# Values of the band and of the memory as products of 512 weight columns, in weight pieces of two feature tiles

## The chip, the cores and the metric

One core of one Trainium2 chip runs the kernel. The metric is the device time of one execution in microseconds. Three executions of the kernel before gave 1246.0, 1249.38 and 1249.93 us; the median, 1249.38 us, is the time before.

## The reference, cut to what matters

The program is one layer of an encoder trunk for 512 tokens of 1024 features, all in float32. Two token mixers work on the same normalised input h: a gated delta rule with 8 heads (A) and a band attention with 16 heads (B). Their outputs are merged, then follow a cross-attention into 256 memory tokens with 4 heads, a feed-forward part and a last norm. The two products that the change touches are the value projection of the band, and the value half of the memory projection:

```
h = rmsnorm(x, norm_mix[l])
qa, ka, va, za, alpha, beta, qb, kb, vb, ga, gb = _split_cols(h @ w_in[l], IN_SPLITS)   # vb: 512 x 1024
...
ob = _chunk_band_attention(qb, kb, vb, band_bias)
...
kk, vv = _split_cols(memn @ w_kv, (M_HEADS * M_DH, M_HEADS * M_DH))                     # vv: 256 x 1024
```

## The kernel before, in words

**Products.** Each float32 operand is kept as two parts, hi and lo, in a reduced format of the same width, and each product of a feature tile is three matmuls: hi by hi, lo by hi, hi by lo. `split` (L113) makes the parts: ScalarE copies into hi (L114), VectorE or GpSimd subtracts for lo (L116, or L118 with a scale). `weights` (L121) loads a piece of weights with a DMA on SP's queue (raw) and splits it (whi, wlo); each of the three has 3 buffers of 1024 columns, so a piece is at most 512 KB.

Most products are made by `block_steps` (L131): 128 weight columns stand in TensorE, and all 512 tokens move through. The result is transposed, features by tokens. Values are wanted the other way, tokens by features, and are made by `natural` (L149): it loads two pieces of four feature tiles each for 256 output columns, and then for each tile of 128 tokens opens one PSUM bank and makes 8 x 3 matmuls, in which the activations stand and the 256 weight columns move (L165 to L167). After every second feature tile (six matmuls) it yields; after the eighth it hands the bank to `evac`.

**Who uses natural here.** `vb_all` (L654) makes the values of the band: four groups of 256 columns, four token tiles each, so 64 yields. Its evac copies 256 columns with ScalarE into a buffer (vbt, three buffers, tag "c") and writes them to DRAM scratch dvb with a DMA on SP's queue (L659); after `proj_a` they are loaded back. `mem_v` (L890) makes the values of the memory: four groups, two token tiles; its evac splits 256 columns into hi and lo of the tile mv. `z_group` uses natural too and is not part of the change.

**PSUM.** Three tags share the eight banks: "mm" with 3 (PM), "ms" with 2 (PS), "sd" with 3 (PD). A new tile waits until the bank it is given has been read out.

**The order of the work.** TensorE's order is the order of the program text; the other engines' orders and the buffers are laid out by a planner with a simulated timeline. `drive` (L176) runs a generator of products and, at each of its yields, first `advance`s every pending generator by one step, then adds rate to a counter due, which starts at -delay x rate, and makes one step of the side generator for each whole unit in it.

The band values run with the output steps of the eight delta-rule heads as the side (L703): rate 1.5, delay 6. A head (`head_out`, L458) takes seven steps: (1) oU, four matmuls into a PS bank; (2) oS, three matmuls into the other PS bank; (3) ScalarE and VectorE read both out; (4) ScalarE squares and sums; (5) VectorE and GpSimd make the factor f (L483, L484), then two waits (5, 6); (7) VectorE scales four tiles into zs (L489), a DMA brings a gate (L492), and `oa_tile` of the head before (L501) transposes its zs into a PS bank (oaT, L506), which ScalarE (oah) and VectorE (oal, L118) read out. The first head has no oaT and takes six; the last takes six waits more and then its own oaT. Pending beside them are the last parts of q6 and q7 (`q_after`, L431): the convolution that reads the bank of q (three steps on VectorE, L351), nine waits, a step qn with four transposes into a PS bank, a step in which ScalarE squares it (L444) and VectorE makes fe (L446), and a step kq with four matmuls into a PS bank that VectorE reads into PT (L454). Ahead of the band values stand the products q5, q6 and q7, which use the three PM banks in turn; behind them `proj_a` (L809), which uses PM banks and takes its weights w_a, eight pieces, over SP's queue.

The memory values stand between the memory keys (`mk`, products of 256 memory tokens) and the queries of the first cross-attention head (L1039), with no side.

Of the kernel before, what the change touches and what calls it, by code (L numbers as in the profile page):

```python
# [9 lines left out]
F32R = mybir.dt.float32r  # L10
AF = mybir.ActivationFunctionType
# [3 lines left out]
P = 128  # L15
T = 512
D = 1024
KD = 8
NT = 4
# [20 lines left out]
def hybrid_block(  # L40
# [5 lines left out]
    nc = tc.nc  # L46
# [19 lines left out]
    def G(tag, name, dt=F32):  # L66
        return up.tile([P, T], dt, tag=tag, bufs=SLOTS[tag], name=nm(name))
# [6 lines left out]
    def TMP(name, tag, bufs=None, shape=(P, T), dt=F32, pool=None):  # L74
        return (pool or tp).tile(list(shape), dt, tag="t" + tag, bufs=bufs or TB[tag], name=nm(name))
# [37 lines left out]
    def split(hi, lo, src, scale=None, eng=None):  # L113
        nc.scalar.activation(hi, src, AF.Copy, scale=1.0 if scale is None else scale)  # L114
        if scale is None:
            (eng or nc.vector).tensor_tensor(out=lo, in0=src, in1=hi.bitcast(F32), op=ALU.subtract)  # L116
        else:
            nc.vector.scalar_tensor_tensor(out=lo, in0=src, scalar=scale, in1=hi.bitcast(F32),  # L118
                                           op0=ALU.mult, op1=ALU.subtract)
# [29 lines left out]
    def natural(src, width, act, ntok, evac, eng=None):  # L149

        w = [weights(src[hf], 4, width, eng) for hf in range(2)]
        for tt in range(ntok):
            ps = PM("nat")
            for k in range(KD):
                natural_step(ps, w[k // 4], k % 4, width, act, tt, k)
                if k % 2:
                    yield
            evac(tt, ps)

    def natural_step(ps, w, kw, width, act, tt, k):  # L160
        tok = slice(tt * P, (tt + 1) * P)
        hi, lo = w
        xh, xl = act[k]
        o = ps[:, :width]
        nc.tensor.matmul(out=o, lhsT=xh[:, tok], rhs=hi[:, kw, :], start=(k == 0), stop=False)  # L165
        nc.tensor.matmul(out=o, lhsT=xl[:, tok], rhs=hi[:, kw, :], start=False, stop=False)  # L166
        nc.tensor.matmul(out=o, lhsT=xh[:, tok], rhs=lo[:, kw, :], start=False, stop=(k == KD - 1))  # L167

    pending = []

# [5 lines left out]
    def drive(*items, side=None, delay=0, rate=1.0):  # L176

        due = -delay * rate
        for steps, after in items:
            for _ in steps:  # L180
                advance()
                due += rate
                while side is not None and due >= 1:
                    due -= 1
                    next(side, None)
            if after is not None:
                pending.append(after)
        if side is not None:
            for _ in side:
                advance()  # L190
# [267 lines left out]
    def head_out(hd):  # L458

        on, ss = kT[hd], SM("ss", 4)  # L460
        pu_, pq = PS("oU"), PS("oS")
        for n in range(NT):
            c = slice(n * P, (n + 1) * P)
            nc.tensor.matmul(out=pu_[:, c], lhsT=PT[hd][:, c], rhs=vs[hd][:, c], start=True, stop=True)
        yield
        for n in range(1, NT):
            c = slice(n * P, (n + 1) * P)
            nc.tensor.matmul(out=pq[:, c], lhsT=qT[hd][:, c], rhs=S[hd, n - 1], start=True, stop=True)
        yield
        for n in range(NT):  # L470
            c = slice(n * P, (n + 1) * P)
            if n > 0:
                nc.scalar.activation(on[:, c], pq[:, c], AF.Copy, scale=eG[:, n, hd : hd + 1])
            else:
                nc.scalar.activation(on[:, c], pu_[:, c], AF.Copy)
        nc.vector.tensor_tensor(out=on[:, P:], in0=pu_[:, P:], in1=on[:, P:], op=ALU.add)
        yield
        for n in range(NT):
            junk = TMP("junk", "junk", 2, (P, P), pool=ap)
            nc.scalar.activation(junk, on[:, n * P : n * P + P], AF.Square, accum_out=ss[:, n : n + 1])  # L480
        yield
        f = SM("f", 4)
        nc.vector.scalar_tensor_tensor(out=f, in0=ss, scalar=4.0 / P, in1=fe[hd], op0=ALU.mult, op1=ALU.add)  # L483
        nc.gpsimd.tensor_tensor(out=f, in0=f, in1=mhalf, op=ALU.pow)  # L484
        yield from wait(2)
        z = zs[hd // 2]
        zc = slice((hd % 2) * P, (hd % 2) * P + P)
        for n in range(NT):
            nc.vector.scalar_tensor_tensor(out=z[:, n, zc], in0=on[:, n * P : (n + 1) * P], scalar=f[:, n : n + 1],  # L489
                                           in1=z[:, n, zc], op0=ALU.mult, op1=ALU.mult)  # L490
        s = sga[hd] = G("b", "sga")
        nc.sync.dma_start(out=s, in_=dga[hd])  # L492
        if hd:
            yield from oa_tile(hd - 1)
        if hd == AH - 1:
            yield from wait(6)
            yield from oa_tile(hd)
# [154 lines left out]
    vb = []  # L652

    def vb_all():  # L654
        for g in range(4):
            def ev(tt, ps, g=g):
                v = TMP("vbt", "c")[:, :256]
                nc.scalar.activation(v, ps[:, 0:256], AF.Copy)
                nc.sync.dma_start(out=dvb[tt, :, g * 256 : g * 256 + 256], in_=v)  # L659
            yield from natural(wvb[g], 256, h, NT, ev)  # L660

    def z_group(g):
        yield from natural(wz[g - 1], 256, xg if g <= 1 else h, NT, z_evac(g), nc.gpsimd if g > 1 else None)
# [1 line left out]
    def seq(*gens):  # L665
        for g in gens:
            yield from g
# [32 lines left out]
    lo_eng[0] = nc.gpsimd  # L700
    go("q3 q4 q5 q6 q7", side=states(), rate=1.0, delay=0)
    lo_eng[0] = nc.vector
    drive((vb_all(), None), side=seq(*[head_out(hd) for hd in heads]), rate=1.5, delay=6)  # L703
    flush()
    inner.__exit__(None, None, None)
    ap_ctx.__exit__(None, None, None)
# [183 lines left out]
    def mem_v(groups):  # L890
        for g in groups:
            for tt in range(2):
                mv[tt][g] = G("b", "mv", F32R)
            def ev(tt, ps, g=g):
                v = mv[tt][g]
                split(v[:, 0:256], v[:, 256:], ps[:, 0:256], stat["mem"][:, tt : tt + 1])
            yield from natural(w_mv[g], 256, mg, 2, ev)


    y, bps = [], {}  # L900
# [135 lines left out]
        opened[j] = PM("mo")  # L1036
        yield from block_steps(opened[j], w_mo[j], ox)

    drive((mem_v(range(4)), None), (queries(0), None))  # L1039
    for hd in range(3):  # L1040
        drive((queries(hd + 1), None), side=cross(hd), delay=3, rate=0.8)
    drive((mo_open(), seq(*[mo_after(j) for j in range(3)])), side=cross(3), delay=3, rate=0.8)
# [89 lines left out]
def _layout(inputs):  # L1132
    import numpy as np

    a = {k: np.asarray(v) for k, v in inputs.items()}

    def blocks(w):
        kt, nb = w.shape[0] // P, w.shape[1] // P
        return np.ascontiguousarray(w.reshape(kt, P, nb, P).transpose(2, 1, 0, 3))

    def groups(w, width):
        ng = w.shape[1] // width
        return np.ascontiguousarray(w.reshape(2, 4, P, ng, width).transpose(3, 0, 2, 1, 4))

    def feat(g):
        return g.reshape(-1, P).T

    w_in = a["w_in"][0]
    col = lambda o: w_in[:, o : o + D]
    r = {}  # L1150
    r["xT"] = np.ascontiguousarray(a["x"][0].T.reshape(KD, P, T))
    r["memT"] = np.ascontiguousarray(a["mem"][0].T.reshape(KD, P, MEM).transpose(1, 0, 2))
    cw = a["conv_w"][0].reshape(4, 24, P).transpose(2, 1, 0).reshape(P, 96)
    rep = lambda v: np.broadcast_to(v.reshape(1, -1), (P, v.size))
    r["consts"] = np.ascontiguousarray(np.concatenate([
        feat(a["norm_mix"][0]), feat(a["norm_xattn"][0]), feat(a["norm_mem"][0]), feat(a["norm_ffn"][0]),
        feat(a["norm_final"]), feat(a["head_norm"][0]), rep(a["a_log"][0]), rep(a["dt_bias"][0]), cw], axis=1))
    z0 = np.concatenate([w_in[:, 4096:4112], w_in[:, 3072:3328]], axis=1)
    r["wz0"] = groups(z0, 272)[0]
    r["wz"] = groups(w_in[:, 3328:4096], 256)  # L1160
    r["wq"], r["wk"], r["wv"] = blocks(col(0)), blocks(col(1024)), blocks(col(2048))
    r["wqb"], r["wkb"] = blocks(col(4112)), blocks(col(5136))
    r["wvb"] = groups(col(6160), 256)
    r["wga"], r["wgb"] = blocks(col(7184)), blocks(col(8208))
    r["w_a"], r["w_b"] = blocks(a["w_a_out"][0]), blocks(a["w_b_out"][0])
    f = np.pad(a["rel_bias"], ((0, 0), (64, 255)), mode="edge")[:, ::-1]
    i = 127 - np.arange(P)[:, None] + np.arange(T)[None, :]
    r["bias"] = np.ascontiguousarray(f[:, i])
    r["w_o"], r["w_mq"] = blocks(a["w_o"][0]), blocks(a["w_mq"][0])
    r["w_mk"] = blocks(a["w_mkv"][0][:, :D])  # L1170
    r["w_mv"] = groups(a["w_mkv"][0][:, D:], 256)
    r["w_mo"] = blocks(a["w_mo"][0])
    r["w_g"], r["w_u"] = blocks(a["w_gate_up"][0][:, :FF]), blocks(a["w_gate_up"][0][:, FF:])
    r["w_d"] = blocks(a["w_down"][0])
    return r
# [24 lines left out]
```

## Time and profile before

| | |
|---|---|
| median of three runs | 1249.38 us |
| the profiled execution | 1248.53 us |
| its span, first to last instruction | 1246.6 us |
| mean granted clock of TensorE | 0.994 |
| band values, first product to the next stage's first | 309.24 to 378.44 us |
| memory values, the same | 727.54 to 750.58 us |

The profile is of one execution. PE is TensorE's matmuls, PEld its weight loads (which overlap them), DVE VectorE, ACT ScalarE, POOL GpSimd, SP the queue of SyncE that issues most DMAs. A row of the timeline has the start in us, the length, the engine, the line of the code, the operation, what it writes and reads by the program's names, the shape, and in brackets how long its engine had stood idle and what ended that. A plain float32 matmul counts as two instructions (oU: x8 for four). Matmul lengths overlap: a matmul of 256 columns has a length of 0.28 us though the next one starts 0.12 us later, so what counts is the distance between starts. A row of the windows has start and end, length, then busy time and count of instructions for each engine, the granted clock, the DMA engines' busy share and GB/s. A row of the waits has who waited, for whom, the sum in us, how many times, and the longest.

### The profile page before, as it was taken

How to read it: one execution, taken by the hardware profiler on the slowest of the kernel's cores; microseconds unless marked ns; L12 is line 12 of the kernel's file. 1: busy time of each engine (PE TensorE's matmuls, PEld its weight loads, DVE VectorE, ACT ScalarE, POOL GpSimd, SP SyncE). 2: the span in 40 equal slices, each digit the busy share in tenths (PEclk: the TensorE clock that was granted, in tenths of full speed). 3: DMA queues.
4: the chain of work that ended last, by engine and by line, in shares of the span. 5: the costliest groups of instructions: out<-in, count | busy, mean ns of one | idle time of the engine just before them, and what ended most of it. 6: DMA issues, size and time to landing. Idle time of an engine off the chain costs nothing.

```text
span 1246.6 us, 17768 instructions
## 1 busy us (share of the span) xinstructions
PE 1220.3 (98%) x6899; PEld 1029.2 (83%) x6899; DVE 687.6 (55%) x1277; ACT 528.2 (42%) x1042; POOL 190.6 (15%) x153
## 2 busy tenths in 40 slices
PE   8899999999999999999999999999999999999997
PEld 7788787889998887777788998888888888888887
DVE  6998894447543388885366564545434344332234
ACT  6544334355652366675323443443323223222232
POOL 4444121130110000001122200004111111110000
PEclk9999999999999999999999999999999999999999
DMA  6253334211344432223334453113232333323343
GB/s 207 70 147 111 114 123 124 68 60 51 119 124 137 156 110 87 92 77 94 101 92 130 127 177 110 52 51 118 85 102 86 101 93 93 102 76 100 103 114 124
DMA packets 60372, 131.07 MB, mean 105 GB/s; under 512 B 17632, under 2 KB 26240, under 8 KB 60288
## 3 DMA queue, kind: packets, MB, share of 16 engines
q1 hardware_dynamic: 59200, 128.89, 33.9%
q8 instruction: 54, 0.88, 0.3%
q10 hardware_dynamic: 1088, 1.05, 0.2%
q14 instruction: 30, 0.25, 0.1%
HBM read 122.04 MB, written 7.88 MB: 104 GB/s over the span
## 4 chain that ended last, share of the span: by engine, by line
PE 84%; DVE 7%; issue 3%; ACT 2%; DMA 2%; POOL 1%; SPq 0%; POOLq 0%; DVEq 0%; ACTq 0%
PE ff L140 7%; PE ff L141 7%; PE ff L142 7%; PE g L140 5%; PE g L142 5%; PE g L141 5%; PE nat L165 2%; PE nat L166 2%; PE nat L167 2%; PE pt L779 2%; PE ob L787 2%; DVE conv L351 1%; PE kb L140 1%; PE gb L140 1%; PE qb L140 1%
## 5 line engine op out<-in xcount | busy, mean ns | idle before, releaser
L114 ACT ACTIVATE whi<-raw 128x1024 fp32r<-128x1024 f32 (+3 forms) x205 | 212.2, 1036 | 467.2 <-PE ff L141 158.4
L116 DVE TENSOR_TENSOR wlo<-raw,whi 128x1024 fp32r<-128x1024 f32 (+2 forms) x188 | 236.2, 1257 | 144.7 <-ACT whi L114 141.9
L140 PE MATMUL ff<-xh,whi 128*128 128x512 f32 x352 | 139.1, 395 | 0.0
L142 PE MATMUL ff<-xh,wlo 128*128 128x512 f32 x352 | 138.9, 395 | 0.0
L141 PE MATMUL ff<-xl,whi 128*128 128x512 f32 x352 | 138.9, 395 | 0.0
L206 POOL TENSOR_TENSOR acc<-acc,sq 128x512 f32<-128x512 f32 (+1 forms) x33 | 47.1, 1427 | 312.1 <-ACT sq L205 180.4
L140 PEld LDWEIGHTS ff<-xh,whi 128*128 128x128 f32 x352 | 66.3, 188 | 15.5
L142 PEld LDWEIGHTS ff<-xh,wlo 128*128 128x128 f32 x352 | 66.3, 188 | 15.5
L141 PEld LDWEIGHTS ff<-xl,whi 128*128 128x128 f32 x352 | 66.3, 188 | 15.3
L1068 POOL TENSOR_TENSOR fa<-fa,rrow 128x512 f32<-128x512 f32 x22 | 39.0, 1772 | 199.0 <-ACT fa L1067 193.8
L116 POOL TENSOR_TENSOR wlo<-raw,whi 128x1024 fp32r<-128x1024 f32 x17 | 41.3, 2432 | 120.9 <-ACT whi L114 120.9
L1071 DVE TENSOR_TENSOR fb<-ff,fa 128x512 f32<-128x512 f32 x22 | 15.2, 692 | 76.4 <-PE ff L142 73.7
L165 PE MATMUL nat<-whi,hh 128*128 128x256 f32 x192 | 57.2, 298 | 0.0
L167 PE MATMUL nat<-wlo,hh 128*128 128x256 f32 x192 | 54.2, 282 | 0.1
L166 PE MATMUL nat<-whi,hl 128*128 128x256 f32 x192 | 54.2, 282 | 0.0
L142 PE MATMUL g<-guh,wlo 128*128 128x512 f32 x132 | 51.4, 390 | 0.0
L141 PE MATMUL g<-gul,whi 128*128 128x512 f32 x132 | 51.4, 390 | 0.0
L140 PE MATMUL g<-guh,whi 128*128 128x512 f32 x132 | 51.4, 390 | 0.0
L1066 DVE TENSOR_TENSOR fa<-ff,rrow 128x512 f32<-128x512 f32 x22 | 15.2, 691 | 61.0 <-PE ff L142 59.5
L763 ACT ACTIVATE P<-P,mx 128x128 f32<-128x128 f32 (+1 forms) x64 | 35.8, 560 | 29.4 <-DVE mx L761 29.2
L165 PEld LDWEIGHTS nat<-whi,hh 128*128 128x128 f32 x192 | 36.7, 191 | 0.8
L166 PEld LDWEIGHTS nat<-whi,hl 128*128 128x128 f32 x192 | 36.7, 191 | 0.1
(380 smaller groups left out, 3147.8 us busy)
## 6 DMA issues: line engine op xcount, KB each, us to landing
raw<-in_w_g SPq DMA_DIRECT2D x22, 512.0 KB, 3.6
raw<-in_w_u SPq DMA_DIRECT2D x22, 512.0 KB, 3.5
raw<-in_w_d SPq DMA_DIRECT2D x20, 512.0 KB, 3.5
raw<-in_wk SPq DMA_DIRECT2D x8, 512.0 KB, 3.7
raw<-in_wga SPq DMA_DIRECT2D x8, 512.0 KB, 3.5
raw<-in_wv SPq DMA_DIRECT2D x8, 512.0 KB, 3.6
raw<-in_wq SPq DMA_DIRECT2D x8, 512.0 KB, 3.6
raw<-in_wvb SPq DMA_DIRECT2D x8, 512.0 KB, 3.6
```

The costliest lines, as they stand in the source:

```text
L114: nc.scalar.activation(hi, src, AF.Copy, scale=1.0 if scale is None else scale)
L116: (eng or nc.vector).tensor_tensor(out=lo, in0=src, in1=hi.bitcast(F32), op=ALU.subtract)
L140: nc.tensor.matmul(out=ps[:, :w], lhsT=hi[:, k - a, :], rhs=xh[:, n], start=first, stop=False)
L141: nc.tensor.matmul(out=ps[:, :w], lhsT=hi[:, k - a, :], rhs=xl[:, n], start=False, stop=False)
L142: nc.tensor.matmul(out=ps[:, :w], lhsT=lo[:, k - a, :], rhs=xh[:, n], start=False, stop=last)
L165: nc.tensor.matmul(out=o, lhsT=xh[:, tok], rhs=hi[:, kw, :], start=(k == 0), stop=False)
L166: nc.tensor.matmul(out=o, lhsT=xl[:, tok], rhs=hi[:, kw, :], start=False, stop=False)
L167: nc.tensor.matmul(out=o, lhsT=xh[:, tok], rhs=lo[:, kw, :], start=False, stop=(k == KD - 1))
L206: nc.gpsimd.tensor_tensor(out=acc, in0=acc, in1=sq, op=ALU.add)
L763: nc.scalar.activation(pr, pr, AF.Exp, scale=-1.0, bias=mx, accum_out=rs[:, t : t + 1])
L779: nc.tensor.transpose(out=pt[:, (t - kt) * P : (t - kt + 1) * P], in_=Pr[p, hh, t][:, kt * P : kt * P + P], identity=ident)
L1068: nc.gpsimd.tensor_tensor(out=a, in0=a, in1=row3, op=ALU.mult)
```

## The change

A new function `wide` makes a product of 512 output columns. It opens one PSUM bank for each token tile at once, then goes through the weights in four pieces of two feature tiles and 512 columns (again 512 KB); for each piece it goes through all token tiles, makes 2 x 3 matmuls in each, and yields. The last piece ends with the evac of each tile. `vb_all` and `mem_v` use it, with two groups instead of four; their evacs take 512 columns, the copy of band values in one instruction and one DMA, the memory values in the same two splits of 256 as before. The banks of the band values are PM, PM, PM, PD in the first group and PD, PD, PM, PM in the second; those of the memory values PM, PM. The side of the band values goes at rate 3.0 with delay 3, as a yield now stands for six matmuls of 512 columns and there are 32 of them. The weights are laid out in DRAM on the host in the order of the pieces.

```diff
+    def wide(src, act, banks, evac):
+
+        ps = [b("wide") for b in banks]
+        for q in range(4):
+            hi, lo = weights(src[q], 2, T)
+            for tt in range(len(ps)):
+                tok = slice(tt * P, (tt + 1) * P)
+                for i in range(2):
+                    k = 2 * q + i
+                    xh, xl = act[k]
+                    nc.tensor.matmul(out=ps[tt], lhsT=xh[:, tok], rhs=hi[:, i, :], start=(k == 0), stop=False)
+                    nc.tensor.matmul(out=ps[tt], lhsT=xl[:, tok], rhs=hi[:, i, :], start=False, stop=False)
+                    nc.tensor.matmul(out=ps[tt], lhsT=xh[:, tok], rhs=lo[:, i, :], start=False, stop=(k == KD - 1))
+                yield
+                if q == 3:
+                    evac(tt, ps[tt])
...
     def vb_all():
-        for g in range(4):
+        for g in range(2):
             def ev(tt, ps, g=g):
-                v = TMP("vbt", "c")[:, :256]
-                nc.scalar.activation(v, ps[:, 0:256], AF.Copy)
-                nc.sync.dma_start(out=dvb[tt, :, g * 256 : g * 256 + 256], in_=v)
-            yield from natural(wvb[g], 256, h, NT, ev)
+                v = TMP("vbt", "c")
+                nc.scalar.activation(v, ps, AF.Copy)
+                nc.sync.dma_start(out=dvb[tt, :, g * T : g * T + T], in_=v)
+            yield from wide(wvb[g], h, ((PM, PM, PM, PD), (PD, PD, PM, PM))[g], ev)
...
-    drive((vb_all(), None), side=seq(*[head_out(hd) for hd in heads]), rate=1.5, delay=6)
+    drive((vb_all(), None), side=seq(*[head_out(hd) for hd in heads]), rate=3.0, delay=3)
...
             for tt in range(2):
-                mv[tt][g] = G("b", "mv", F32R)
+                for x in range(2):
+                    mv[tt][2 * g + x] = G("b", "mv", F32R)
             def ev(tt, ps, g=g):
-                v = mv[tt][g]
-                split(v[:, 0:256], v[:, 256:], ps[:, 0:256], stat["mem"][:, tt : tt + 1])
-            yield from natural(w_mv[g], 256, mg, 2, ev)
+                for x in range(2):
+                    v = mv[tt][2 * g + x]
+                    split(v[:, 0:256], v[:, 256:], ps[:, 256 * x : 256 * x + 256], stat["mem"][:, tt : tt + 1])
+            yield from wide(w_mv[g], mg, (PM, PM), ev)
...
-    drive((mem_v(range(4)), None), (queries(0), None))
+    drive((mem_v(range(2)), None), (queries(0), None))
...
+    def wides(w):
+        return np.ascontiguousarray(w.reshape(4, 2, P, -1, T).transpose(3, 0, 2, 1, 4))
...
-    r["wvb"] = groups(col(6160), 256)
+    r["wvb"] = wides(col(6160))
...
-    r["w_mv"] = groups(a["w_mkv"][0][:, D:], 256)
+    r["w_mv"] = wides(a["w_mkv"][0][:, D:])
```

## The prediction

> **What bounds the kernel now.** I read the page first: the span, the engines' busy time and the chain of work that ended last.
>
> ```profile
> span 1246.6 us, 17768 instructions
> ...
> PE 1220.3 (98%) x6899; PEld 1029.2 (83%) x6899; DVE 687.6 (55%) x1277; ACT 528.2 (42%) x1042; POOL 190.6 (15%) x153
> ...
> PE 84%; DVE 7%; issue 3%; ACT 2%; DMA 2%; POOL 1%; SPq 0%; POOLq 0%; DVEq 0%; ACTq 0%
> ```
>
> TensorE is busy for 98% of the span and makes 84% of the chain, so a microsecond of matmul issue saved is a microsecond of the end, unless a wait takes its place. Busy time of overlapping matmuls is no pace, so next I took the two stages that change by windows from their first matmul to the next stage's first, for the tile of their products alone (core, window, length, then PE busy and count).
>
> ```profile
> 309.24:378.44 69.20, 51.53 (x384) 47.40 (x383) 0.00 (x0) 5.67 (x15) 1.00 0.38 114
> 727.54:750.58 23.04, 23.04 (x192) 23.00 (x192) 3.37 (x7) 3.26 (x7) 1.00 0.60 181
> ```
>
> Memory values: 192 matmuls of 256 columns in 23.04 us, 0.1200 us from start to start, with no gap. Band values: 384 of them, 46.1 us at that pace, in a stage of 69.2 us; the other 23 us are the delta-rule heads worked off between them (head_out, and what is pending of q), and waits. The waits of TensorE in that window say which:
>
> ```profile
> PEld oS L468 <- DVE PT L454: 1.4, 1, 1.4
> PEld oaT L506 <- issue: 1.4, 1, 1.4
> PEld oS L468 <- DVE oal L118: 0.9, 3, 0.4
> ```
>
> 3.7 us of waits, all at instructions of the heads, none at weights. So the weights' path (DMA, ScalarE's split, VectorE's remainder) has slack here, and the question is what 512 columns cost, and what the heads' new places cost.
>
> **The change, part by part.** *The pace.* 384 matmuls of 256 columns become 192 of 512, and 192 become 96. Two quiet stretches of 512-column products give the pace (the fourth number is the weight loads, one for each matmul; they count the starts):
>
> ```profile
> 381.19:391.39 10.20, 10.20 (x46) 8.45 (x45) 3.58 (x4) 2.12 (x2) 0.24 (x2) 1.00 0.56 189
> 752.67:763.83 11.16, 11.16 (x50) 9.04 (x48) 3.56 (x5) 3.09 (x4) 0.00 (x0) 1.00 0.42 140
> ```
>
> The first (proj_a, moving tiles from the main pools) gives 10.20/45 = 0.2267 us, the second (queries, moving tiles from the late pool) 11.16/48 = 0.2325. Two of 256 take 0.2400. What moves now is whi and wlo, from a main pool, so I take 0.2267 and keep 0.2325 as the upper end. A pair saves 13.3 ns (7.5 at the other end): 192 x 13.3 = 2.56 us in band values and 96 x 13.3 = 1.28 in memory values, 3.84 us together (2.16 at the other end). This is all that the change can gain by columns: the gain is only the fixed part of a matmul, since columns streamed stay the same.
>
> The Trainium skill, page "TensorE: Matmul & The Clock Gate", section "Back-to-back issue gap", puts the isolated warm gap at N/2.4 + 2.5 ns; that would save one 2.5 ns in each pair, 0.7 us over 288 pairs instead of 3.84. The trace differs: 120.0 ns at 256 columns is 13 ns above 256/2.4, so here the rows decide.
>
> *The places of the side steps.* drive used to call 1.5 side steps after each six 256-column matmuls, and now calls three after each six 512-column ones: the same steps per microsecond, in bigger bundles. Fewer bundles mean fewer changes between kinds of matmul. The price of each, from TensorE's timeline:
>
> ```profile
> 315.59 1.05 PE L464 MATMUL oU<-vs,PT 128*128 128x128 f32 x8
> 316.40 0.36 PE L165 MATMUL nat<-whi,hh 128*128 128x256 f32 x1
> 316.60 0.28 PE L166 MATMUL nat<-whi,hl 128*128 128x256 f32 x1
> ...
> 327.26 0.60 PE L506 MATMUL oaT<-ident,zs 128*128 128x128 f32 x4
> 327.61 0.36 PE L165 MATMUL nat<-whi,hh 128*128 128x256 f32 x1
> ```
>
> oU takes 0.81 us, oaT 0.35, and the first product after a bundle is followed after 0.20 us instead of 0.12: a return costs 0.08. Counting bundles in the timeline before gives 23; with step s of the side (three from yield 4 on, seven steps a head) falling after yield 4 + (s-1)/3, and the pending q parts after yields 2, 4, 10 and 12, there are 15. Eight returns fewer are 0.64 us; three more changes from transposes to plain matmuls inside a bundle give about 0.25 back. Net -0.4 us.
>
> *Waits that appear.* PS has two banks and three users per head (oU, oS, oaT), so inside a bundle a third user waits for the first to be read out. The distances that this takes:
>
> ```profile
> 322.06 1.06 PE L451 MATMUL kq<-qT,kT 128*128 128x128 f32 x8
> 324.34 0.94 PE L468 MATMUL oS<-L,qT 128*128 128x128 f32 x6 [1.22 <-DVE PT L454]
> ...
> 344.10 0.60 PE L506 MATMUL oaT<-ident,zs 128*128 128x128 f32 x4
> ...
> 345.25 1.06 PE L464 MATMUL oU<-vs,PT 128*128 128x128 f32 x8
> 346.26 0.94 PE L468 MATMUL oS<-L,qT 128*128 128x128 f32 x6
> ```
>
> From kq to an oS in its bank 2.28 us, from oaT to an oS in its bank 2.16. After yield 4 stand kq of head 6, oU and oS of head 0: 2.28 less two blocks of 0.81 leaves 0.7 us of waiting. After yields 8 and 15 stand oaT, oU and oS (heads 0, 2, 2 and 3, 5, 5): 2.16 less 0.35 and 0.81 is 1.0 each. After yield 10 stand qn of head 7, oaT and oU of head 3, whose bank is qn's:
>
> ```profile
> 310.68 0.60 PE L439 MATMUL qn<-ident,qT 128*128 128x128 f32 x4
> ```
> ```profile
> 312.30 0.22 ACT L444 ACTIVATION_READ_ACCUMULATOR junk<-qn 128x1 f32 x1
> ```
>
> The squares let go of qn 1.84 us after its start; less two blocks of 0.35 and a change, 1.0. The old wait at kq of head 7 (1.4) goes: it stands after yield 12 with only oaT behind it. The other new wait is at the start. wide opens a bank for each of four token tiles; the third is the bank of q7, which natural reached only after two whole tiles. VectorE reads q7 out here:
>
> ```profile
> 310.36 1.23 DVE L116 TENSOR_TENSOR wlo<-raw,whi 128x1024 fp32r<-128x1024 f32 x1 [1.94 <-ACT whi L114]
> 311.50 0.74 DVE L351 SCALAR_TENSOR_TENSOR conv<-qa,cst,conv 128x511 f32<-128x511 f32 x1
> 312.55 0.17 DVE L446 TENSOR_SCALAR fe<-sq 128x4 f32<-128x4 f32 x1 [0.31 <-ACT junk L444]
> 312.63 1.52 DVE L351 SCALAR_TENSOR_TENSOR conv<-qa,cst,conv 128x510 f32<-128x510 f32 x2
> ```
>
> The new third tile is reached at 309.24 + 12 x 0.2267 + 0.35 (qn) = 312.3; q7 is read out at 314.15, or, as fe comes later in the new order, at 311.50 + 3 x 0.74 = 313.7. I take 1.4 us (0 if the three conv steps go ahead of wlo, 1.9 as they stand). Behind that wait stand all later matmuls; ScalarE and VectorE go on. At the end, oaT of head 7 waited for zs, which waited for f on GpSimd behind four memsets:
>
> ```profile
> 357.86 0.83 PE L468 MATMUL oS<-L,qT 128*128 128x128 f32 x6
> ...
> 360.68 0.60 PE L506 MATMUL oaT<-ident,zs 128*128 128x128 f32 x4
> ```
> ```profile
> 361.33 0.52 POOL L715 MEMSET klz<- 64x512 f32 x1 [4.34 <-PE oaT L506]
> ...
> 363.54 1.00 POOL L484 TENSOR_TENSOR f<-f,mhalf 128x4 f32<-128x4 f32 x1
> ```
>
> The memsets start once oaT of head 6 is done. It now comes two yields after the end of oS of head 7 (2 x 1.44 us; before 2.2, as oS takes 0.6), late enough for f to be ahead of them: 0.2 us (0 to 1.4) instead of 1.4. Sum of waits: 1.4 + 0.7 + 1.0 + 1.0 + 1.0 + 0.2 = 5.3 against 3.7: +1.6 us (from -1.4, if the first two are covered and the planner keeps the banks clear, to +4).
>
> *What costs nothing while its cover holds.* Weights: as many pieces (8 and 8) of as many bytes; each is now used once for all tiles, 24 matmuls or 5.4 us in band values, and 12 or 2.72 us in memory values (before 2.88):
>
> ```profile
> L658 ACT ACTIVATE vbt<-nat x16: 358/383/390, 312.7 to 379.5; 128x256 f32<-128x256 f32 x16
> ```
> ```profile
> raw<-in_w_mv SPq DMA_DIRECT2D x8, 512.0 KB, 3.5
> ```
> ```profile
> GB/s 207 70 147 111 114 123 124 68 60 51 119 124 137 156 110 87 92 77 94 101 92 130 127 177 110 52 51 118 85 102 86 101 93 93 102 76 100 103 114 124
> ```
>
> 512 KB (524288 bytes) in 2.72 us is 193 GB/s; the kernel's own start moves 207 for a whole slice, and at that rate a piece takes 2.5 us, so three buffers keep up; if only 181 GB/s came, as now, the stage would stay at 23.04 us and 1.28 us of gain be lost. The 16 read-outs of 383 ns become 8 wider ones, and 16 writes of 128 KB on SP become 8 of 256 KB. The last four bunch at the end of each group; behind them on SP stand w_a's pieces, needed 5.4 us apart, so they have room. In memory values the two splits per tile stay; each has a bank to itself for 2.7 us.
>
> *Sum*: -3.84 - 0.4 + 1.6 = -2.6 us. The profiled execution took 1248.53 us (span 1246.6 and 1.9 around it), which gives 1245.9. The median of the three runs is 1249.38, 0.85 higher: 1246.8. About 0.3%, 3.7 us, is what a measurement can tell here.
>
> **The rivals.** *Waits covered* (chance 0.27): the planner orders ScalarE and VectorE anew, and the waits fall to 2.3 us, 1.4 below now: -3.84 - 0.4 - 1.4 = -5.6, 1243.8. For it: all heads' results before came in time but two, and VectorE is busy half of the stage. Against: oaT, oU and oS in one bundle leave nothing between them.
>
> *The bundles stall every head* (0.12; slower). Place: PS's two banks in band values. If a read-out of a value tile is put ahead of oah on ScalarE (0.7 us, an estimate: under twice vbt's 383 ns), oaT's bank comes as much later, and if oU and oS of all eight heads meet a taken bank, each pays 1.0 + 0.7: 13.6 with 2.1 for the start and kq is 15.7, 12 above now, so -4.2 + 12 = +7.8, 1257. It decides from waits of 11.7 us on (3.7 + 4.2 + 3.7). Against: by the count of yields only three of eight heads meet a taken bank.
>
> *The columns bring nothing* (0.09): whi as a moving tile of 512 is slower than the late pool's tiles, 0.2375 us, so a pair saves 2.5 ns and 288 of them 0.7 us: -0.7 - 0.4 + 1.6 = +0.5, 1249.9. Nothing shows such a pace; but no 512-column product here moves a weight tile. The skill's gap formula named above would give this saving.
>
> **How the numbers follow.** The forecast has 0.52, nearly all within 0.3% (0.04 of it beyond, where the waits are few); with *columns bring nothing* 0.57 for the same. Faster: 0.27 + 0.04 = 0.31. Slower: 0.12. The range: downwards to *waits covered* and a little, 1243.4; upwards the slow pace and waits of +3: -2.16 - 0.4 + 3.5 = +0.9, with *columns bring nothing* 1250.6. Outside are the stalled heads and some 0.06.
>
> **What would show it.** In the profile after: memory values in 21.8 us from the first to the last product and no idle PE (22.3 says the slow pace, 23 that it is bound by weights); products of 512 columns in band values 0.227 us apart between bundles; a wait at the third token tile's first product for conv, one at oS or oU after yields 4, 8, 10 and 15 for PT, oal and junk, each about 1 us; no wait at oaT of head 7; band values in 69.2 - 2.56 - 0.4 + 1.6 = 67.8 us. It is wrong if the waits of TensorE in that stage sum to under 2.5 us or over 9, or if a later stage loses time, where I have put none.

## The result, and the profile after

The median of seven runs is 1252.13 us (1251.22 to 1256.48), beside 1248.5 us (1246.0 to 1249.93) for the kernel before on the same chip. The ratio is 1.0038 with an interval of [1.0023, 1.0054]: slower by about 4.7 us (2.9 to 6.7). The ratio is estimated from all executions and is not the quotient of the two medians, which are 3.6 us apart. The forecast of 1246.8 us and its whole range, 1243.4 to 1250.6, lie below the median. The profiled execution was the slowest of the seven, 1256.48 us. First the page of the kernel after: span and busy time.

```profile
span 1254.4 us, 17164 instructions
...
PE 1219.7 (97%) x6611; PEld 1015.8 (81%) x6611; DVE 687.6 (55%) x1277; ACT 527.7 (42%) x1034; POOL 190.2 (15%) x153
```

The 288 matmuls fewer are there (6899 before), and TensorE is still busy for 97% of the span: the page alone doesn't tell what happened. The windows by stage of the kernel after do: a stretch ahead of the change, the band values, all between, the memory values (columns as in the prediction, without the filter by tile).

```profile
188.00:219.00 31.00, 29.31 (x518) 23.46 (x517) 10.95 (x18) 14.45 (x29) 4.78 (x2) 0.89 0.43 117
311.74:385.84 74.10, 66.31 (x361) 55.95 (x360) 34.99 (x78) 40.55 (x138) 10.10 (x12) 0.98 0.34 101
385.84:734.93 349.09, 349.09 (x1777) 282.61 (x1776) 214.15 (x449) 169.27 (x329) 31.35 (x40) 1.00 0.38 113
734.93:758.29 23.36, 22.05 (x98) 17.95 (x97) 12.61 (x15) 10.96 (x15) 0.00 (x0) 1.00 0.62 179
```

The band values grew from 69.20 to 74.10 us, the memory values from 23.04 to 23.36. Between them nothing changed: 349.09 us, and before 727.54 - 378.44 = 349.10. The start, 311.74 instead of 309.24, is 2.5 us late with code that is the same there; in the first window the granted clock was 0.89. That belongs to this execution: in another execution of the same kernel (*e1_again* below) the band values start at 308.22 and take 72.69 us. So in that execution, beside the profile of before, the two stages are slower by 3.5 + 0.3 = 3.8 us. The waits of TensorE in the band values of the kernel after (the first two columns name who waited and for whom; its line numbers of the heads are 17 above those of before):

```profile
PEld oS L485 <- DVE oal L118: 4.2, 3, 2.8
PEld oU L481 <- ACT junk L461: 1.7, 1, 1.7
PEld wide L179 <- ACT junk L461: 1.6, 1, 1.6
PEld oaT L523 <- PE wide L181: 1.4, 1, 1.4
PEld oS L485 <- DVE PT L471: 0.5, 1, 0.5
```

9.4 us against 3.7 before. All are waits for a PSUM bank but the fourth. The third is the first product of the third token tile. The list names ScalarE's squares of qn (junk), which end within 0.01 us of VectorE's last read of q7 (conv); TensorE's timeline of the kernel after names conv. The fourth is put down to the product before it; there the timeline has VectorE's zs as what ended it:

```profile
316.45 0.47 PE L179 MATMUL wide<-whi,hh 128*128 128x512 f32 x1 [1.39 <-DVE conv L368]
...
374.04 1.03 PE L523 MATMUL oaT<-ident,zs 128*128 128x128 f32 x4 [0.99 <-DVE zs L506]
```

The largest is 2.8 us, at the bundle after yield 8 (2.8 in the weight loads, which the list counts; 2.56 in the matmuls, which the timeline shows). On TensorE of the kernel after it looks so (start, length, line, in brackets the idle time before):

```profile
327.79 0.39 PE L181 MATMUL wide<-wlo,hh 128*128 128x512 f32 x1
...
329.18 0.39 PE L181 MATMUL wide<-wlo,hh 128*128 128x512 f32 x1
329.40 0.60 PE L523 MATMUL oaT<-ident,zs 128*128 128x128 f32 x4
329.84 1.06 PE L481 MATMUL oU<-vs,PT 128*128 128x128 f32 x8
333.46 1.65 PE L485 MATMUL oS<-L,qT 128*128 128x128 f32 x6 [2.56 <-DVE oal L118]
...
335.33 0.63 PE L180 MATMUL wide<-whi,hl 128*128 128x512 f32 x1
...
336.61 0.40 PE L180 MATMUL wide<-whi,hl 128*128 128x512 f32 x1
```

oS takes the bank that oaT has just filled. It starts 4.06 us after oaT, where the prediction took 2.16. What the two engines that read oaT out did meanwhile, ScalarE of the kernel after first:

```profile
329.37 1.06 ACT L114 ACTIVATE whi<-raw 128x1024 fp32r<-128x1024 f32 x1
330.34 0.67 ACT L114 ACTIVATE oah<-oaT,cst 128x512 fp32r<-128x512 f32 x1
```

Then VectorE of the kernel after:

```profile
330.47 1.22 DVE L116 TENSOR_TENSOR wlo<-raw,whi 128x1024 fp32r<-128x1024 f32 x1 [0.95 <-ACT whi L114]
331.61 1.13 DVE L506 SCALAR_TENSOR_TENSOR zs<-kT,f,zs 128x128 f32<-128x128 f32 x4
332.66 0.74 DVE L118 SCALAR_TENSOR_TENSOR oal<-oaT,cst,oah 128x512 fp32r<-128x512 f32 x1
```

A weight piece is split ahead of oah, and the rest of that split and the four scalings into the next zs stand ahead of oal. Each engine takes its work in the order that the planner gave, so oaT's bank waits for work that has nothing to do with it; no single instruction in these rows is out of the ordinary (oah 0.67 us and oal 0.74; 0.69 and 0.75 in the kernel before).

The other two waits for oal show the same distance, from oaT to the oS in its bank, at other places:

```profile
346.25 0.60 PE L523 MATMUL oaT<-ident,zs 128*128 128x128 f32 x4
349.50 0.93 PE L485 MATMUL oS<-L,qT 128*128 128x128 f32 x6 [0.37 <-DVE oal L118]
...
353.03 0.60 PE L523 MATMUL oaT<-ident,zs 128*128 128x128 f32 x4
355.24 0.94 PE L485 MATMUL oS<-L,qT 128*128 128x128 f32 x6 [0.72 <-DVE oal L118]
```

From yield 12 to yield 13 it is 3.25 us; VectorE's reads of kq into PT (346.45) and the rest of a weight split (347.49) stand ahead of oal there. After yield 15 it is 2.21 us, close to what the prediction took; only the read-out of a value tile (353.23) stands ahead of oah there, and no split and no scaling ahead of either. The wait of oU for the squares has the same form, on ScalarE of the kernel after: oah stands ahead of the last of the four squares of qn.

```profile
339.90 0.70 ACT L114 ACTIVATE oah<-oaT,cst 128x512 fp32r<-128x512 f32 x1
340.47 0.29 ACT L461 ACTIVATE junk<-qn 128x128 f32<-128x128 f32 x1
```

The memory values have one wait of 1.7 us, where the prediction had none. TensorE of the kernel after, around the second token tile of the second group:

```profile
746.98 0.39 PE L181 MATMUL wide<-wlo,mg 128*128 128x512 f32 x1
748.67 0.47 PE L179 MATMUL wide<-whi,mg 128*128 128x512 f32 x1 [1.31 <-DVE mv L118]
```

PM has three banks. Group one takes two, group two the third and then the first again, which is being read out in two halves. ScalarE and VectorE of the kernel after over that read-out:

```profile
744.68 0.47 ACT L114 ACTIVATE mv<-wide,mrs 128x256 fp32r<-128x256 f32 x1 [0.53 <-PE wide L181]
745.81 1.06 ACT L114 ACTIVATE whi<-raw 128x1024 fp32r<-128x1024 f32 x1 [0.66 <-DVE mv L118]
746.78 0.82 ACT L114 ACTIVATE mv<-wide,mrs 128x256 fp32r<-128x256 f32 x2
```
```profile
745.33 0.48 DVE L118 SCALAR_TENSOR_TENSOR mv<-wide,mrs,mv 128x256 fp32r<-128x256 f32 x1
746.91 1.23 DVE L116 TENSOR_TENSOR wlo<-raw,whi 128x1024 fp32r<-128x1024 f32 x1 [1.10 <-ACT whi L114]
748.05 0.87 DVE L118 SCALAR_TENSOR_TENSOR mv<-wide,mrs,mv 128x256 fp32r<-128x256 f32 x2
```

Hi of the first half (744.68), lo of it on VectorE (745.33), hi of the second half (746.78), lo of it (748.05): they take turns, with a split of weights between (745.81 and 746.91), and the first token tile's bank is free at about 748.5.

### The profile page after: what moved, and what is told of

Its sections match the earlier page's. It is cut to its first block, busy times and chain, and to the rows that moved or that the text cites. A ratio compares the mean times of both kernels' runs of the same rounds, so it can differ in the third digit from the quotient of the medians.

```text
span 1254.4 us, 17164 instructions
## 1 busy us (share of the span) xinstructions
PE 1219.7 (97%) x6611; PEld 1015.8 (81%) x6611; DVE 687.6 (55%) x1277; ACT 527.7 (42%) x1034; POOL 190.2 (15%) x153
## 4 chain that ended last, share of the span: by engine, by line
PE 84%; DVE 7%; issue 3%; ACT 2%; POOL 1%; DMA 1%; SPq 0%; POOLq 0%; DVEq 0%; ACTq 0%
PE ff L142 7%; PE ff L140 7%; PE ff L141 7%; PE g L140 5%; PE g L142 5%; PE g L141 5%; PE pt L796 2%; DVE conv L368 2%; PE ob L804 2%; PE wide L179 2%; PE wide L180 2%; PE wide L181 1%; PE kb L140 1%; PE gb L140 1%; PE qb L140 1%
## 5 line engine op out<-in xcount | busy, mean ns | idle before, releaser
L778 DVE CUSTOM_DVE_ANT_0 P<-sc,bias 128x128 f32<-128x128 f32 (+1 forms) x64 | 31.0, 485 | 6.5 <-PE pt L796 6.4
L371 ACT ACTIVATE th<-conv 128x512 f32<-128x512 f32 x24 | 15.1, 631 | 34.7 <-DVE conv L368 29.3
L141 PEld LDWEIGHTS g<-gul,whi 128*128 128x128 f32 x132 | 24.8, 188 | 5.3
L140 PEld LDWEIGHTS g<-guh,whi 128*128 128x128 f32 x132 | 24.8, 188 | 5.2
```

The lines of the kernel that those rows point to most:

```text
L140: nc.tensor.matmul(out=ps[:, :w], lhsT=hi[:, k - a, :], rhs=xh[:, n], start=first, stop=False)
L141: nc.tensor.matmul(out=ps[:, :w], lhsT=hi[:, k - a, :], rhs=xl[:, n], start=False, stop=False)
L778: nc.vector.tensor_tensor_reduce(out=pr, in0=ps[:, :W], in1=b[:, T - W :], scale=-1.0, scalar=3e38, op0=ALU.add, op1=ALU.min, accum_out=mx)
```

## The experiments

The theory from the traces: the columns bring what was forecast, and waits for banks take more than all of it; oaT's bank in PS is the main one. The rivals: the bundles of three steps cost by themselves, whatever the bank; the columns bring nothing; or the loss is in the execution and not in the kernel. The stage lengths below run from a stage's first product to the next stage's first, in each kernel's profile, so each is from one execution; where two kernels have the same stage and the same granted clock, they differ by at most 0.07 us. Each ratio is to the kernel before on the same chip (medians 1248.44 us beside e1 to e4, 1248.04 beside e5 to e8, 1248.65 beside e10 to e13), so ratios are compared and not medians.

| kernel | band values, us | waits in them, us | memory values, us | median, us | ratio to before |
|---|---|---|---|---|---|
| before | 69.20 | 3.7 | 23.04 | 1248.5 | |
| after (e1_again) | 72.69 | 9.4 | 23.38 | 1253.02 | 1.0037 [1.0024, 1.005] |
| e2_band_only | 72.71 | 9.4 | 23.04 | 1251.9 | 1.0029 [1.0018, 1.004] |
| e3_memory_only | 69.22 | 3.7 | 23.38 | 1248.94 | 1.0004 [0.9994, 1.0014] |
| e4_bundles_only | 77.95 | 9.7 | 23.04 | 1256.61 | 1.0067 [1.0053, 1.0082] |
| e5_single_steps | 72.06 | 8.5 | 23.36 | 1251.53 | 1.0029 [1.0018, 1.004] |
| e6_oat_bank | 66.44 | 3.5 | 23.36 | 1245.63 | 0.9976 [0.9967, 0.9986] |
| e7_first_banks | 71.31 | 8.2 | 23.36 | 1251.76 | 1.0029 [1.0018, 1.004] |
| e8_memory_banks | 72.64 | 9.4 | 21.79 | 1252.18 | 1.0027 [1.0018, 1.0036] |
| e12_before_oat_bank | 68.21 | 2.7 | 23.04 | 1247.22 | 0.9978 [0.9966, 0.999] |
| e13_bundles_256_oat | 67.20 | 1.8 | 23.04 | 1246.56 | 0.9982 [0.9973, 0.999] |
| e11_bundles_repaired | 65.12 | 2.3 | 21.78 | 1243.7 | 0.9959 [0.9946, 0.9971] |
| e10_single_repaired | 69.05 | 5.1 | 21.79 | 1247.15 | 0.998 [0.9971, 0.999] |

**The kernel after once more, and each half of the change alone.** The first is the kernel after without an edit.

> The changed kernel unaltered, once more, to part what belongs to it from what belongs to one execution. Stages are taken from the first product of one to the first of the next. Waits theory: the places of the waits are fixed by the program, so band values again take 74.1 us within 0.5 with waits of 9 to 10 us on TensorE's loads, memory values 23.4 us, and the 2.5 us that the first profile lost ahead of the band values (granted clock 0.89 in one window) do not come back; time 1250 to 1252 us, 3 to 5 above before. Clock theory (the loss is a clock that drops at random): the band values come out anywhere from 70 to 76 us.

In the second, the memory values are made by `natural` again, with four groups.

```diff
-            yield from wide(w_mv[g], mg, (PM, PM), ev)
+            yield from natural(w_mv[g], 256, mg, 2, ev)
```

> Only the band values are changed; the memory values stay as before (256 columns, four groups). Waits theory: all of the loss is here; band values 74.1 us as in the changed kernel, memory values 23.04 us as before; +4.9 us against the kernel before (+4 to +5.5). Columns theory (512 moving weight columns are the loss wherever they stand): about two thirds of the loss, +3.

In the third, the band values are, at the old rate.

```diff
-            yield from wide(wvb[g], h, ((PM, PM, PM, PD), (PD, PD, PM, PM))[g], ev)
+            yield from natural(wvb[g], 256, h, NT, ev)
...
-    ..., rate=3.0, delay=3)
+    ..., rate=1.5, delay=6)
```

> Only the memory values are changed; the band values stay as before. Waits theory: the columns gain 1.28 us and the wait for the bank of the first token tile of the first group gives 1.6 back, so memory values 23.4 us and the time +0.3 us, not to be told from before. Columns theory: a third of the loss, +1.5 us.

The loss is repeated (1.0037), with the same waits to a tenth. The length of the band values was missed: 72.69 and 72.71 us, where 74.1 was expected in both kernels. The 1.4 us more belong to the first execution, where TensorE ran slowly behind the longest wait (last section). In e1_again the granted clock of the stage is 1.00, and the stage is still 3.5 us longer than before, so the clock isn't the cause of the loss. The halves add up within their intervals: 0.0029 and 0.0004 beside 0.0037. The loss is the band values'; the memory half alone cannot be told from no change.

**The bundles without the columns.** The kernel before with 256 columns, a yield after every four feature tiles, and the side at the new rate, so the same three steps stand together as in the kernel after.

```diff
-                if k % 2:
+                if k % every == every - 1:
                     yield
...
-            yield from natural(wvb[g], 256, h, NT, ev)
+            yield from natural(wvb[g], 256, h, NT, ev, every=4)
...
-    ..., rate=1.5, delay=6)
+    ..., rate=3.0, delay=3)
```

> The kernel before with 256 columns everywhere; only the band values yield half as often (after twelve matmuls instead of six) and the side goes at rate 3.0 with delay 3, so the side steps stand in the bundles of the changed kernel. Waits theory: the bundles alone bring the waits for the two banks of the heads (oS for oal after yields 4, 8 and 15, oU for the squares after yield 10), so band values 72 to 74 us, +3 to +5 us, without the wait for the third token tile's bank. Columns theory: as before, 69.2 us within 0.5.

77.95 us, 8.75 above before and more than the 72 to 74 that were expected. The largest line of TensorE's waits in this kernel:

```profile
PEld oS L468 <- DVE oal L118: 6.1, 2, 3.2
```

The others are 1.7 for the squares, 1.4 at the last oaT and 0.5 for PT: the list of the kernel after, without the wait at the third token tile and with more for oal. The waits are 6.0 us more than before (9.7 less 3.7). The other 2.8 us are a slower pace: the granted clock of the stage is 0.96, and behind both waits for oal the products of 256 columns are for a while 0.213 us apart instead of 0.120. The median lies 8.2 us above before on that chip, about as much as the stage does in the profile. So the new places of the steps cost without any wide product. The stage is 5.3 us shorter in e1_again, but about half of that is the slow pace, so this pair doesn't price the columns.

**The steps in ones and twos again, as before.** The kernel after with a yield after each feature tile and the old rate.

```diff
                     nc.tensor.matmul(out=ps[tt], lhsT=xh[:, tok], rhs=lo[:, i, :], start=False, stop=(k == KD - 1))
-                yield
+                    yield
...
-    ..., rate=3.0, delay=3)
+    ..., rate=1.5, delay=6)
```

> The changed kernel, but wide yields after each feature tile (three matmuls of 512 columns) and the side goes at rate 1.5 with delay 6, so the heads' steps stand as far apart in time as before the change. Waits theory: the waits of the changed kernel at oS and oU (4.2 + 1.7 us) fall back to those of the kernel before (0.9 for oal, 1.4 for PT), the wait for the third token tile's bank stays (1.6); band values 69.2 - 2.6 + 0.5 (pace between bundles 0.231 us, not 0.227) + 1.6 = 68.7 us, the time 0 to 1 us under before. Columns theory: band values stay over 71 us.

A miss: 72.06 us, hardly below the kernel after. The waits went elsewhere, as the view of this kernel shows:

```profile
PEld oaT L523 <- issue: 2.9, 1, 2.9
PEld oS L485 <- DVE oal L118: 2.5, 5, 0.9
PEld oS L485 <- DVE PT L471: 1.4, 1, 1.4
```

Three smaller ones sum to 1.7. oal is down from 4.2 to 2.5 and not to 0.9, and the last oaT waits 2.9. On GpSimd of this kernel, f, which its zs needs, stands behind all four memsets (the first of them, then f):

```profile
362.81 0.52 POOL L732 MEMSET klz<- 64x512 f32 x1 [5.33 <-ACT junk L497]
...
365.03 1.00 POOL L501 TENSOR_TENSOR f<-f,mhalf 128x4 f32<-128x4 f32 x1
```

f stood behind the memsets in the kernel before too, but there they began 0.65 us after the oaT ahead of them (360.68); here they began 1.85 us after it (360.96), once ScalarE's squares of the last head were done. Another 1.5 us of the stage are a slow pace behind that wait (last section). The part of the theory by which spreading the steps as before brings the old waits back fell with this: the same places of the steps came with another order on the other engines.

**The bank of oaT.** The kernel after with oaT in a PD bank.

```diff
-        pt = PS("oaT")
+        pt = PD("oaT")
```

> The changed kernel with bundles of three as they are, but the transposes of a head's result (oaT) go to a PD bank instead of a PS bank, so that only two users share the two PS banks. Waits theory: the 4.2 us at oS for oal go, the wait at oU for the squares (1.7) falls to under 0.5 as the other bank is free; band values 67.5 to 68.5 us; time 0 to 1 us under before, unless oaT now meets a PD bank that a token tile holds. Clock or order theory (bundles cost by their kind, not by the bank): no change from 72.7 us.

66.44 us, 6.25 below e1_again, and the kernel is faster than before: 0.9976 [0.9967, 0.9986]. Its waits:

```profile
PEld wide L179 <- ACT junk L461: 1.6, 1, 1.6
PEld oaT L523 <- PE wide L181: 1.4, 1, 1.4
PEld oS L485 <- DVE PT L471: 0.5, 1, 0.5
```

The waits for oal and for the squares are gone, 5.9 us. It is the bank, with the bundles as they were. How much of the gain over the kernel before is the bank's alone, e12_before_oat_bank tells below.

**The other two banks.** In the first of these kernels the third token tile takes a PD bank and the fourth the third PM bank; in the second the two token tiles of the second memory group take PD banks.

```diff
-            yield from wide(wvb[g], h, ((PM, PM, PM, PD), (PD, PD, PM, PM))[g], ev)
+            yield from wide(wvb[g], h, ((PM, PM, PD, PM), (PD, PD, PM, PM))[g], ev)
```

> The changed kernel, but the first group of band values takes its banks as PM, PM, PD, PM, so that the bank of q7 is wanted for the fourth token tile and not for the third. Waits theory: the wait of 1.6 us for conv at the third tile falls to 0.2 or less, the other waits stay; band values 71.2 us against 72.7, time about 1.5 us under the changed kernel.

```diff
-            yield from wide(w_mv[g], mg, (PM, PM), ev)
+            yield from wide(w_mv[g], mg, ((PM, PM), (PD, PD))[g], ev)
```

> The changed kernel, but the second group of memory values opens two PD banks, so that none of its tiles waits until the first group has been read out. Waits theory: memory values 21.8 us (96 times 0.2267) instead of 23.4, the rest as in the changed kernel: time 1.5 us under it. If the weights' path bounds the stage (512 KB in 2.72 us), it stays at 23 us or shows waits for wlo.

In the first, the wait at the new tile falls from 1.6 to 0.4 us and the stage by 1.38, to 71.31, so it was the bank of q7. In the second, the memory values fall to 21.79 us. The window of the memory values in that kernel:

```profile
727.33:749.12 21.79, 21.79 (x98) 18.03 (x97) 12.52 (x15) 10.86 (x15) 0.00 (x0) 1.00 0.61 193
```

TensorE is busy throughout, and 193 GB/s arrive: the weights keep up, as forecast, once the bank is free. The ratios of the two kernels (1.0029 and 1.0027) are too near to e1_again's to show either gain by themselves; the stages show it.

**What the columns and the bundles are worth with the banks free.** Three kernels on one chip, in the order of the texts below: the kernel before with oaT in PD; *e4_bundles_only* with oaT in PD; the kernel after with all three banks changed (e11). The edits are those above.

> The kernel before, 256 columns and old places of the steps, with oaT in a PD bank and nothing else. It tells how much of the gain of the repaired kernel is the bank and not the columns. Waits theory: the waits for oal (0.9 us) go, that for PT (1.4) goes or halves, the last oaT's (1.4) stays: band values 67.0 to 68.3 us, 1 to 2 us under before.

> Bundles of three with 256 columns, as the bundles-only kernel, but with oaT in a PD bank. Beside the same repair of the changed kernel (band values 66.4 us, 1.6 of them the wait for q7's bank) it gives the columns' worth with equal places. Waits theory: the bundles' loss of 8.7 us goes, and the columns are worth 2.0 to 2.6 us: band values 67.0 to 67.5 us. If bundles cost by their kind and not by the banks, band values stay above 72.

> The changed kernel with the three repairs that each moved its own wait: oaT in a PD bank, the first group's banks as PM, PM, PD, PM, the second group of memory values in two PD banks. Waits theory: the repairs add up; band values 72.7 - 6.3 - 1.4 = 65.0 us, memory values 21.8, so 4.2 + 1.25 = 5.4 us under the kernel before, ratio 0.9957. If the banks are now short elsewhere (three PD banks for two or three token tiles, oaT and the heads), band values come out above 66.

First the window of the band values with 256 columns and bundles (e13), then those of e11:

```profile
308.99:376.19 67.20, 65.76 (x553) 64.86 (x552) 33.77 (x78) 40.82 (x145) 10.09 (x12) 1.00 0.39 118
```
```profile
309.37:374.49 65.12, 63.80 (x361) 54.35 (x360) 34.62 (x78) 40.15 (x138) 10.10 (x12) 1.00 0.40 112
723.62:745.40 21.78, 21.78 (x98) 18.03 (x97) 12.51 (x15) 10.85 (x15) 0.00 (x0) 1.00 0.65 193
```

Columns alone: 67.20 - 65.12 = 2.1 us, or 2.6 when the 0.5 us more of waits (2.3 against 1.8) are taken out, and 23.04 - 21.78 = 1.26 in the memory values. Bundles alone: 77.95 to 67.20 by the bank, and then 1.0 below the same kernel with the old places of the steps (68.21), nearly all of it waits (1.8 against 2.7). So *columns bring nothing* and *bundles cost whatever the bank* are both out. e11 beats both kernels: 1243.7 us. But the bank alone, without the change, has brought the kernel before to 0.9978 (e12), as far as e6_oat_bank got with the change (0.9976). Beside e12 the change with all its banks repaired (e11) is worth 3.1 us in the band values (68.21 - 65.12) and 1.26 in the memory values.

**Steps in ones and twos with all three banks.** e11 with a yield after each feature tile and the old rate, as in *e5_single_steps*.

> The three repairs with the yields after each feature tile (three matmuls) and the side at rate 1.5, delay 6, so steps stand singly. Waits theory: with the banks free, the places matter little: band values 64.5 to 66.5 us, some 0.6 more than in bundles for eight more returns (0.08 each), and the last oaT waits 1.4 to 2.9 us for zs behind four memsets on GpSimd and a weight split, which no bank repairs.

A miss again: 69.05 us. Its waits are 2.9 at the last oaT, 1.4 at oS for PT, 0.6 at kq and 0.2 at qn; oaT is in a PD bank here, so these have nothing to do with its old bank; e11 differs only in the places of the steps and has 1.4, 0.5 and 0.4 instead. The slow pace stands behind the wait of 2.9 here too.

## Why the prediction was wrong

**The columns were right.** Forecast 2.56 and 1.28 us; 2.1 to 2.6 and 1.26 with the banks free. Just behind a bundle, products of 512 columns are 0.232 us apart in the kernel after (six of them from 327.79 to 329.18), nearer to the upper end of the two rows than to the one taken; in the memory values, 21.78/96 = 0.2269. No wait for weights is in the lists, and no time was lost between the two stages: 349.09 us.

**Most places of the waits were right, several sizes were not.** The measured column is e1_again's; the kernel after has the same to a tenth. Sums are of unrounded waits.

| wait, us | before | forecast | measured |
|---|---|---|---|
| third token tile, for q7's bank | 0 | 1.4 | 1.6 |
| oS for PT, after yield 4 | 1.4 | 0.7 | 0.5 |
| oS for oal, after yield 8 | 0 | 1.0 | 2.8 |
| oS for oal, after yield 15 | 0 | 1.0 | 0.9 |
| oS for oal, elsewhere | 0.9 | 0 | 0.6 |
| oU for the squares, after yield 10 | 0 | 1.0 | 1.7 |
| last oaT | 1.4 | 0.2 | 1.4 |
| sum | 3.7 | 5.3 | 9.4 |
| memory values, second tile of group two | 0 | 0 | 1.7 |

The step that failed is "2.16 less 0.35 and 0.81 is 1.0 each". 2.16 us was the distance from oaT to oS in one bundle of the kernel before, a place where nothing stood ahead of the two read-outs. It was carried to other places as if it belonged to the instructions; it goes with what is queued on ScalarE and VectorE there. With a split and four scalings ahead it was 4.06 after yield 8; with PT and a split ahead it was 3.25 at the bundle after yield 13, where no wait was forecast; with a value tile's read-out ahead, the very work that the slower rival named, it was 2.21 after yield 15, and there the forecast of 1.0 was right (0.9). The same goes for the squares after yield 10: with oah among them the wait was 1.7 instead of 1.0. The slower rival had this mechanism, a piece of other work ahead of oah, and priced it only at all eight heads together; "only three of eight heads meet a taken bank" was taken as evidence against it. One place was enough to make the wait 2.8 instead of 1.0. The forecast's own end of +4 us for the waits lay below the +5.7 that came, their sum of 9.4 lies beyond the 9 that the prediction gave as a sign of being wrong, and the chance of 0.12 for *bundles stall every head* was too small for a mechanism that needs only one bad order.

The second failure is "late enough for f to be ahead of them": the last oaT waited as long as before. That was a guess at GpSimd's order from a shift of 0.7 us (2 x 1.44 less 2.2). The shift came, but in the kernel after VectorE's part of f ended at 370.38 us and the memsets had begun at 370.29, so f stood behind them again. The third is "each has a bank to itself for 2.7 us" in the memory values: the banks were not counted. Three banks and two groups of two tiles mean that the second group's second tile meets the first group's first, and its read-out of two halves took until 748.5. There the columns' 1.26 us were lost to 1.7.

**The sum.** Against before, e1_again's band values should be 69.20 + 5.7 (waits) - 2.6 (columns) - 0.1 (bundles) = 72.2; 72.69 was measured. Bundles bring that 0.1 us beside their waits (1.0 less 0.9 from e12 to e13), not the 0.4 that was put for fewer changes between kinds of matmul. Where the 0.5 us that are left went is open. The whole loss by the runs, 4.7 us [2.9, 6.7], and by the stages, 3.8, agree within the interval. The measured waits put into the prediction's own sum, -3.84 - 0.4 + 5.7 + 1.7 = +3.2 us, give a loss within that interval too. The range had no room for them: its upper end speaks of waits of +3 and is added up with +3.5.

**Open.** That the bank makes these waits is shown by moving it. That their length is set by what is queued ahead of the read-out is read from the timelines and was not tested by an experiment: the bank was moved, not the order. Why the planner put the split ahead of oah, and whether another due time would have moved it, was not tried.

## What to carry to other kernels

In this kernel the wait of a matmul for a bank followed what was queued on the engines that read the bank out (2.2 to 4.1 us from oaT to oS), and not the read-out alone. So a distance measured at one place need not hold at another: price it once more with one piece of the usual work of each such engine ahead. Before work is bundled, count the banks of its tag against the users in a bundle and against the next group's tiles; giving one user another tag (oaT in PD) turned a loss of 0.37% into a gain of 0.24% with a one-word edit. Try such an edit on the kernel before as well: alone it gained 0.22% there, so most of that gain was not the change's. And when an edit has a clear gain (columns) and a clear risk (places), an experiment with the places alone tells in one run whether the places cost anything by themselves.

## What the runs showed of the hardware

After the wait of 2.56 us in the kernel after, TensorE ran at about half pace: from 335.33 to 336.61 three products take 0.427 us each instead of 0.23, and oS in front of them has 1.65 us instead of 0.94. The same wait in e1_again ended otherwise:

```profile
329.96 0.94 PE L485 MATMUL oS<-L,qT 128*128 128x128 f32 x6 [2.56 <-DVE oal L118]
330.65 0.48 PE L179 MATMUL wide<-whi,hh 128*128 128x512 f32 x1
330.97 0.39 PE L180 MATMUL wide<-whi,hl 128*128 128x512 f32 x1
```

That is the difference between their stages, 74.10 and 72.69 us. In e5_single_steps and in e10_single_repaired 2.53 us of idle at the last oaT brought it too, with a granted clock of 0.60 (e5) and 0.57 (e10) over the 4 us behind; in e5:

```profile
367.52:371.50 3.98, 3.98 (x13) 3.18 (x14) 1.39 (x4) 0.69 (x1) 0.00 (x0) 0.60 0.49 136
```

So a wait of 2.5 us can cost 1.4 to 1.5 us more behind it, in some executions and not in others. In the profiles of e4, e5 and e10 (longest waits 3.2, 2.9 and 2.9 us in the lists) the stage has a granted clock of 0.96 to 0.98; in those of e2, e7 and e8 (2.8 us, as in the kernel after) it has 1.00, and so it has in those of e6, e11, e12 and e13 (none over 1.6 us). The Trainium skill, page "TensorE: Matmul & The Clock Gate", section "What's actually happening", has the clock halved after an idle window of some 3.4 us that runs free of the kernel, and in the section "Wait — 56ns, not 53.3ns?" 426.7 ns from start to start at 512 columns while cold. The trace agrees in the pace (0.427 us) and in that it differs between executions; the idle time that was enough here is shorter, 2.53 us.
